# Seven-product units in single-bank PSUM tiles, hi parts one step earlier, and token-factor steps moved: a decoder layer on one core

## The chip, the cores and the metric

The kernel runs on one core of a Trainium2 chip. The metric is device time in microseconds (us) of one execution; lower is better. Three executions of the kernel before took 945.07, 948.32 and 948.42 us, so the median is 948.32 us. The profile shown here is of a fourth execution of the same program.

## What is computed

One layer of a hybrid decoder (`DEPTH = 1`) for 512 prompt tokens and 8 sample tokens that share weights, all in fp32. The mixer sub-layer joins sliding-window attention, a state-space branch and attention to 256 memory tokens. The channel sub-layer, where the change lies, is

```python
h  = rmsnorm(x, norm_ffn_g)
a  = h @ w_ffn_gate                     # 1024 -> 2816
up = h @ w_ffn_up                       # 1024 -> 2816
c  = conv_b + sum(conv_w[j] * a[t - 2 + j] for j in range(3))   # causal, along the tokens
x  = x + (gelu(c) * up) @ w_ffn_down    # 2816 -> 1024
y  = rmsnorm(x, norm_final_g)
```

## The kernel before, in words

Activations lie features by tokens: 128 features on the partitions and 520 columns, in two halves of 260 (256 prompt tokens and 4 sample tokens each). Each fp32 operand is cut into two fp32r parts, hi and lo, and each product of a 128x128 weight block with a 260-column half is three matmuls (`mm3`): hi by hi, hi by lo, lo by hi. For weights ScalarE (ACT) writes the hi part (tiles `whi`) and VectorE (DVE) then takes it from the raw weight for the lo part (`wlo`).

The channel sub-layer has three stretches.

**Plain blocks** (`for ob in range(6)`): gate (`fg`) and up (`fu`) blocks of 128 output features, 48 matmuls each, into a two-bank tile `mm` (pool `pmm`, 2 tiles). DVE moves the gate product to SBUF, the lane `conv` does the three-tap convolution (ACT, two DVE steps, small POOL steps, Gelu on ACT), and DVE then multiplies the up product in. Beside this a filler lane `y_lane` builds the token factors: four calls of `build`, each some ten DVE steps and four ACT copies, which make the four slots of sums and differences of token blocks that the next stretch multiplies by. `pump` lets a filler piece go when the planner's clocks (class `Clock`: costs by engine, plus `LAT` between engines) say that there is room; `MARG_FF` and `EV_FF` set how much, once `clk.late` is set.

**Seven-product units** (class `Strassen`, 16 of them, `fg3`, `fu3` to `fg10`, `fu10`, each for a pair of output blocks): the two output blocks by two token halves by two halves of the features are made with seven block products in place of eight. Each of the seven steps is 12 matmuls (4 factor slots by 3) into one of three accumulators:

```python
ORDER = (("A11", 0, 0, True), ("s1", 3, 2, True), ("s2", 4, 0, False), ("s4", 2, 2, False), ("s3", 5, 0, False),
         ("A12", 1, 1, True), ("A22", 6, 0, False))      # weight, token factor, accumulator, first
...
t = out_tile()
self.acc = [t[:, 0, :NH], t[:, 1, :NH], SD()[:, :NH]]
```

So accumulators 0 and 1 are the two banks of one `mm` tile and accumulator 2 is a bank of the pool `psd` (tiles `SD`, 4 of one bank). After every step `evict` adds the accumulator to where it belongs (table `EVICT`: ACT copies it out where it is the first to arrive, DVE adds or subtracts it where something is there already): A11, s1 and s2 by ACT, s4, s3 and A12 by DVE, A22 by ACT. Accumulator 0 goes on accumulating after it has been read.

**Down steps** (class `Down`), the product with `w_ffn_down` in four groups `d0` to `d3`, stand between the units by the table `FF_ORDER`. The last four blocks of `d3` run half by half at the end, beside the final norm (`finish`).

All steps of the last two stretches form one list. `s_step(s)` emits, in this order: the eviction of step s-1, the split of step s+3 (`s_split(s + D)`: ACT's hi part, DVE's lo part, then the DMA loads that this frees), and the matmuls of step s with filler pieces between them (`spump`). An engine's queue is in order, so what stands in front of a waiting instruction decides who waits. Weights come by DMAs on SP's queue, one part (`S`) also by accumulating DMAs of POOL.

Of the kernel before, what the change touches and what calls it, by code (L numbers as in the profile page):

```python
# [7 lines left out]
F32 = mybir.dt.float32  # L8
# [3 lines left out]
OP = mybir.AluOpType  # L12
# [101 lines left out]
class Clock:  # L114
# [75 lines left out]
    def op(self, eng, name, a, k):  # L190
        outs = [a[0]] + ([k["accum_out"]] if "accum_out" in k else [])
        ins = [x for x in list(a[1:]) + list(k.values()) if hasattr(x, "ap") and x is not outs[-1]]
        shape = a[0].shape
        n = 1
        for d in shape[1:]:
            n *= d
        if eng == "sp":
            out, src = a
            n = 4
            for d in out.shape:  # L200
                n *= d
            t0 = max(self.t["sp"], self.deps(eng, [out], [src]))
            self.t["sp"] = t0 + 0.45
            self.t["hw"] = max(self.t["hw"], t0 + SP_A) + max(0.26, n / 360e3)
            self.note(eng, [out], [src], self.t["hw"] + SP_B)
            return
        if eng == "pe":
            if name == "transpose":
                c = 0.9e-3 * a[1].shape[0] + 0.003
            else:  # L210
                m, w = 1, 1
                for d in a[1].shape[1:]:
                    m *= d
                for d in a[2].shape[1:]:
                    w *= d
                c = (max(0.112, 0.4434e-3 * w + 0.0045) if self.late else 0.417e-3 * max(m, w) + 0.003) \
                    if a[1].dtype == F32R else 1.667e-3 * w * (1 if m > 64 else 0.5)
        elif eng == "act":
            c = 0.833e-3 * n + 0.094 * (1 + sum(hasattr(k.get(x), "ap") for x in ("bias", "scale", "accum_out")))
            if a[1].space == PSUM:  # L220
                c -= 0.043
        elif eng == "dve":
            if name == "tensor_reduce":
                n = 1
                for d in a[1].shape[1:]:
                    n *= d
            c = 0.07 + (6.3e-3 if name == "reciprocal" else 0.52e-3 if name == "tensor_copy" and a[1].space != PSUM
                        else 1.04e-3) * n
            if name == "tensor_tensor_reduce" or name == "scalar_tensor_tensor" and hasattr(a[2], "ap"):
                c += 0.06  # L230
        elif eng == "dma":
            c = 3.3
        else:
            c = {"tensor_tensor": 0.151 + 1.95e-3 * n, "tensor_scalar": 0.215, "memset": 0.035 + 0.833e-3 * n}.get(name, 0.12 + 3.3e-3 * n)
        q = "pool" if eng == "dma" else eng
        t0 = max(self.t[q], self.deps(eng, outs, ins))
        if eng == "pe" and t0 < COLD:
            c *= 2
        end = t0 + c
        self.t[q] = t0 + 1.1 if eng == "dma" else end  # L240
        self.note(eng, outs, ins, end)
        if eng != "dma":
            self.last = max(self.last, end + self.LAT)
        else:
            self.last_dma = end
# [25 lines left out]
EV = 1.5  # L271
HZ = 2.0
EVH = 1.2
MARG_FF = -0.2
EV_FF = 1.5
MARG = -0.4
MARG_Q = -0.2
SP_A, SP_B, COLD = 1.2, 1.0, 10.0
# [11 lines left out]
def body(ctx, tc, I, O):  # L290
# [1296 lines left out]

    clk.late = True  # L1590
    pool.dma_start(O["sk"][:, :127 * 128], I["ckn"][:, 128:])
    pool.dma_start(O["sv"][:, :127 * 128], I["cvn"][:, 128:])
    B_done(2)
# [141 lines left out]
    class Strassen:  # L1735
# [18 lines left out]
                sp.dma_start(t[:, o:o + 512], s_dram(self.n, COL["A21"], 512))  # L1754
            later.append((s, lambda: pool.dma_start(t[:, 0:1024], s_dram(self.n, 512, 1024), accum_op=OP.add)))

        def split(self, p, s):
            name = ORDER[p][0]
            w = self.A(name)
            if name == "s2":  # L1760
                dve.tensor_tensor(w, w, self.A("A11"), op=OP.add)
                if self.nxt:
                    self.nxt.load("A11", s)
            elif name == "s4":
                dve.tensor_tensor(w, w, self.A("A12"), op=OP.add)
            parts_of(s, w, 512)
            if self.nxt:
                if name == "s3":
                    self.nxt.load("S", s + S_LAG)
                elif name in ("A12", "A22"):  # L1770
                    self.nxt.load(name, s)
# [18 lines left out]
        def before(self, p):  # L1790
            if p == 0:
                (fg_begin if self.kind == "fg" else fu_begin)(self.o)
                t = out_tile()
                self.acc = [t[:, 0, :NH], t[:, 1, :NH], SD()[:, :NH]]

        def go(self, p, s):
            _, f, bank, first = ORDER[p]
            for k in range(4):
                w = slice(k * P, (k + 1) * P)
                xh, xl = ysl[k].get(f)  # L1800
                mm3(self.acc[bank], HIW[s][:, w], LOW[s][:, w], xh, xl, first and k == 0, k == 3, not first)
                spump(0.36 * (3 - k))

    dcount = [0]

    class Down:
# [11 lines left out]
        def load(self, p):  # L1818
            sp.dma_start(cu[self.at[p] % 4][:, 0:self.q * P], s_dram(self.n, p * self.q * P, self.q * P))

        def split(self, p, s):
            self.steps[p] = s
            parts_of(s, cu[self.at[p] % 4][:, 0:self.q * P], self.q * P)
            j = self.at[p] + 4
            if j < len(dparts):
                dparts[j][0].load(dparts[j][1])

        def before(self, p):
            if p == 0:
                t = out_tile() if self.halves == (0, 1) or self.m % 2 == 0 else self.t0  # L1830
                if self.halves == (0,):

                    downs[self.m - 7 if self.m < 7 else -1].t0 = t
                    self.ps = [t[:, self.m % 2, :NH], None]
                    return
                self.ps = [t[:, h, :NH] for h in range(H)]
                self.both = t[:, :, :NH]

# [58 lines left out]
    steps = [(u, p) for u in units for p in range(u.n_steps)]  # L1897
    HIW, LOW = {}, {}

    def parts_of(s, src, q):  # L1900
        h, l = half("hi", s % 6)[:, 0:q], half("lo", s % 6)[:, 0:q]
        act.activation(h, src, AF.Copy)
        dve.tensor_tensor(l, src, h.bitcast(F32), op=OP.subtract)
        HIW[s], LOW[s] = h, l

    def s_split(s):
        if s < len(steps):
            u, p = steps[s]
            u.split(p, s)

    D, S_LAG = 3, 3

    def spump(rem):

# [11 lines left out]
    def s_step(s):  # L1926
        u, p = steps[s]
        if s:
            v, q = steps[s - 1]
            v.evict(q)  # L1930
        u.before(p)
        while later and later[0][0] <= s:
            later.pop(0)[1]()
        s_split(s + D)
        u.go(p, s)


# [37 lines left out]
    for ob in range(6):  # L1975
# [36 lines left out]
        if ob:  # L2012
            i = begin("fu")
            if ob == 5:
                for s in range(D):
                    s_split(s)
            pu = product(i, range(8), blk(yh, yl))
        drain([l])
        dve.tensor_tensor(hv(c), pu, hv(c), op=OP.mult)
# [72 lines left out]

    todo = finish(0, NH, (NH,))
    next(todo)
    t = None
    for i, m in enumerate((4, 5, 6, 7)):
        d = downs[m - 8]
        if i % 2 == 0:
            t = out_tile()
        d.ps[1] = t[:, i % 2, :NH]  # L2100
        d.go(0, d.steps[0], (1,))
        if m < 7:
            next(todo, None)
            x_add(m, 1)
# [145 lines left out]
```

## Time and profile before

| | us |
|---|---|
| runs of the kernel before (median) | 945.07, 948.32, 948.42 (948.32) |
| the profiled execution | 955.03 |
| its span, first to last instruction | 953.0 |
| TensorE (PE) busy / DVE / ACT / POOL | 886.5 / 603.2 / 406.6 / 151.9 |
| mean granted TensorE clock | 0.975 of full |

Every instruction of the program has line 257, that of the helper that records it, so the rows are told apart by tiles: `T` stands for the SBUF temporaries, `B` for the large buffers, `M`, `wraw`, `sv` for raw weights. A row of the chain or the timeline begins with its start and its length in us. A timeline row ends with the idle time of the engine before it and who ended it. In a wait row stand the total, the count and the longest. In a row of stages stand the stretch, its length, the busy us (and instructions) of PE, weight loads, DVE, ACT and POOL, the granted clock as a share of 2.4 GHz, the DMA share and GB/s. A matmul's end is modelled: it is drawn 0.28 us long, while the next one starts 0.12 us after it.

### The profile page before, as it was taken

How to read it: one execution, taken by the hardware profiler on the slowest of the kernel's cores; microseconds unless marked ns; L12 is line 12 of the kernel's file. 1: busy time of each engine (PE TensorE's matmuls, PEld its weight loads, DVE VectorE, ACT ScalarE, POOL GpSimd, SP SyncE). 2: the span in 40 equal slices, each digit the busy share in tenths (PEclk: the TensorE clock that was granted, in tenths of full speed). 3: DMA queues.
4: the chain of work that ended last, by engine and by line, in shares of the span. 5: the costliest groups of instructions: out<-in, count | busy, mean ns of one | idle time of the engine just before them, and what ended most of it. 6: DMA issues, size and time to landing. Idle time of an engine off the chain costs nothing.

```text
span 953.0 us, 18057 instructions
## 1 busy us (share of the span) xinstructions
PE 886.5 (93%) x7229; PEld 845.7 (89%) x7229; DVE 603.2 (63%) x1099; ACT 406.6 (43%) x797; POOL 151.9 (16%) x392
## 2 busy tenths in 40 slices
PE   9999999998999999999999999798898999899983
PEld 8998989997898998899999999788887988888973
DVE  6887678873276882126656667766676566666545
ACT  6376645453433221323333334345444445445252
POOL 7885300001000003000000101111112011111001
PEclk9999999999899998899999999899999999999987
DMA  7432572247045327052232145544546545540302
GB/s 262 163 100 90 148 166 90 90 137 141 17 136 157 107 89 174 24 185 83 90 110 89 62 125 141 137 113 131 141 109 149 135 119 132 144 112 17 120 12 90
DMA packets 52213, 110.45 MB, mean 116 GB/s; under 512 B 14001, under 2 KB 23649, under 8 KB 51857
## 3 DMA queue, kind: packets, MB, share of 16 engines
q1 hardware_dynamic: 46656, 93.73, 32.6%
q0 software_dynamic: 4240, 14.41, 8.2%
q8 instruction: 57, 0.93, 0.4%
q10 hardware_dynamic: 1232, 1.16, 0.4%
q14 instruction: 28, 0.22, 0.1%
HBM read 104.05 MB, written 6.26 MB: 116 GB/s over the span
## 4 chain that ended last, share of the span: by engine, by line
PE 66%; DVE 15%; ACT 9%; DMA 5%; issue 4%; POOL 1%; SPq 0%; DVEq 0%; ACTq 0%; POOLq 0%
PE mm L257 53%; PE SD L257 13%; DVE T L257 7%; ACT whi L257 5%; DVE wlo L257 4%; DMA wraw<-in_w 4%; ACT T L257 3%; DVE B L257 3%; DVE wraw L257 1%; DMA B<-kd 1%; ACT B L257 1%; POOL B L257 0%; SPq L257 0%; DVE TN L257 0%; DMA kd<-B 0%
## 5 line engine op out<-in xcount | busy, mean ns | idle before, releaser
L257 PE MATMUL mm<-B,whi 128*128 128x260 f32 (+1 forms) x3808 | 712.8, 289 | 48.9 <-DVE T L257 29.4
L257 PEld LDWEIGHTS mm<-B,whi 128*128 128x128 f32 x3808 | 595.4, 191 | 68.1 <-DVE T L257 19.1
L257 PE MATMUL mm<-B,wlo 128*128 128x260 f32 (+1 forms) x1904 | 542.9, 285 | 1.0 <-DVE wlo L257 1.0
L257 PEld LDWEIGHTS mm<-B,wlo 128*128 128x128 f32 x1904 | 364.1, 191 | 1.8 <-DVE wlo L257 1.7
L257 DVE TENSOR_TENSOR wlo<-wraw,whi 128x1024 fp32r<-128x1024 f32 (+1 forms) x149 | 153.5, 1031 | 150.9 <-ACT whi L257 146.4
L257 ACT ACTIVATE whi<-wraw 128x1024 fp32r<-128x1024 f32 (+1 forms) x149 | 133.4, 897 | 98.1 <-DMA wraw<-in_w 39.1
L257 ACT ACTIVATE T<-mm 128x260 f32<-128x260 f32 (+3 forms) x76 | 32.2, 446 | 87.9 <-PE mm L257 87.9
L257 DVE TENSOR_TENSOR wlo<-M,whi 128x512 fp32r<-128x512 f32 x64 | 44.3, 691 | 33.3 <-ACT whi L257 30.8
L257 ACT ACTIVATE B<-T 128x520 fp32r<-128x520 f32 (+2 forms) x48 | 29.7, 620 | 66.2 <-DVE T L257 66.2
L257 PE MATMUL SD<-B,whi 128*128 128x260 f32 x288 | 54.5, 286 | 0.2 <-DVE B L257 0.2
L257 ACT ACTIVATE whi<-M 128x512 fp32r<-128x512 f32 x64 | 39.7, 626 | 23.2 <-DVE M L257 23.2
L257 PE MATMUL SD<-B 128*64 128x72 f32 (+9 forms) x576 | 45.4, 253 | 1.9 <-DMA B<-kd 1.9
L257 PEld LDWEIGHTS SD<-B,whi 128*128 128x128 f32 x288 | 45.3, 192 | 0.4 <-DVE B L257 0.4
L257 DVE TENSOR_TENSOR B<-B 128x256 f32<-128x256 f32 (+11 forms) x78 | 36.4, 474 | 13.4 <-ACT B L257 12.0
L257 ACT ACTIVATE B<-SD 128x256 fp32r<-128x256 f32 (+6 forms) x50 | 19.0, 406 | 59.4 <-PE SD L257 59.3
L257 PEld LDWEIGHTS SD<-B 128*64 128x64 f32 (+5 forms) x576 | 31.6, 130 | 12.6 <-issue 6.1
L257 PE MATMUL SD<-B,wlo 128*128 128x260 f32 x144 | 41.1, 285 | 0.0
L257 DVE SCALAR_TENSOR_TENSOR T<-T,sm,T 128x512 f32<-128x512 f32 x44 | 33.6, 763 | 2.8 <-ACT T L257 2.6
L257 DVE TENSOR_TENSOR B<-mm,B 128x520 f32<-128x520 f32 (+3 forms) x41 | 24.6, 602 | 15.0 <-PE mm L257 15.0
L257 DVE TENSOR_TENSOR T<-T,T 128x520 f32<-128x520 f32 (+2 forms) x50 | 30.3, 606 | 5.1 <-ACT T L257 5.1
L257 POOL MEMSET T<- 128x2 f32 (+2 forms) x27 | 7.7, 285 | 159.8 <-DVE B L257 89.3
L257 DVE TENSOR_TENSOR B<-T,B 128x520 fp32r<-128x520 f32 (+2 forms) x50 | 31.4, 638 | 0.4
(166 smaller groups left out, 828.6 us busy)
## 6 DMA issues: line engine op xcount, KB each, us to landing
wraw<-in_w SPq DMA_DIRECT2D x96, 512.0 KB, 3.6
M<-in_w SPq DMA_DIRECT2D x48, 256.0 KB, 3.8
wraw<-in_w SPq DMA_DIRECT2D x36, 256.0 KB, 3.4
T<-in_w SPq DMA_DIRECT2D x36, 192.0 KB, 3.3
M<-in_w POOLq DMA_DIRECT2D x8, 512.0 KB, 6.1
wraw<-in_w POOLq DMA_DIRECT2D x8, 512.0 KB, 6.4
sv<-in_w SPq DMA_DIRECT2D x12, 192.0 KB, 3.4
B<-in_xT SPq DMA_DIRECT2D x1, 2080.0 KB, 9.4
```

Of the source, the lines that this page charges most:

```text
L257: return g(*a, **k)
```

## The change

It does three things. Accumulator 1 of a unit leaves the second bank of the `mm` tile and becomes an `SD` tile; in the same way the four half-by-half blocks at the end no longer share a tile two by two. `s_split` is cut in three (`sum`, `hi`, `lo`): the sums and the hi part of step s+4 are emitted where before all of step s+3 was; the lo part stays at s+3. And the planner's constants for the channel sub-layer change (`LAT`, ACT and DVE costs, `MARG_FF`, `EV_FF`), which sets filler pieces at other places.

```diff
-            if a[1].space == PSUM:
+            if self.late:
+                c += 0.06
+            elif a[1].space == PSUM:
                 c -= 0.043
...
-            c = 0.07 + (6.3e-3 if name == "reciprocal" else 0.52e-3 if name == "tensor_copy" and a[1].space != PSUM
+            c = (0.15 if self.late else 0.07) + (6.3e-3 if name == "reciprocal" else 0.52e-3 if name == "tensor_copy" and a[1].space != PSUM
...
-MARG_FF = -0.2
-EV_FF = 1.5
+MARG_FF = 1.0
+EV_FF = 4
...
-    clk.late = True
+    clk.late, clk.LAT = True, 0.2
...
-        def split(self, p, s):
+        def sum(self, p, s):
             name = ORDER[p][0]
-            w = self.A(name)
-            if name == "s2":
-                dve.tensor_tensor(w, w, self.A("A11"), op=OP.add)
-                if self.nxt:
+            if name in ("s2", "s4"):
+                w = self.A(name)
+                dve.tensor_tensor(w, w, self.A("A11" if name == "s2" else "A12"), op=OP.add)
+                if self.nxt and name == "s2":
                     self.nxt.load("A11", s)
-            elif name == "s4":
-                dve.tensor_tensor(w, w, self.A("A12"), op=OP.add)
-            parts_of(s, w, 512)
+
+        def hi(self, p, s):
+            hi_of(s, self.A(ORDER[p][0]), 512)
+
+        def lo(self, p, s):
+            name = ORDER[p][0]
+            lo_of(s, self.A(name), 512)
             if self.nxt:
                 if name == "s3":
                     self.nxt.load("S", s + S_LAG)
...
-                t = out_tile()
-                self.acc = [t[:, 0, :NH], t[:, 1, :NH], SD()[:, :NH]]
+                self.acc = [out_tile()[:, 0, :NH], SD()[:, :NH], SD()[:, :NH]]
...
+    def one(m):
+
+        return SD()[:, :NH] if m % 2 else out_tile()[:, 0, :NH]
...
-                t = out_tile() if self.halves == (0, 1) or self.m % 2 == 0 else self.t0
                 if self.halves == (0,):
-
-                    downs[self.m - 7 if self.m < 7 else -1].t0 = t
-                    self.ps = [t[:, self.m % 2, :NH], None]
+                    self.ps = [one(self.m), None]
                     return
+                t = out_tile()
...
-    def parts_of(s, src, q):
-        h, l = half("hi", s % 6)[:, 0:q], half("lo", s % 6)[:, 0:q]
-        act.activation(h, src, AF.Copy)
-        dve.tensor_tensor(l, src, h.bitcast(F32), op=OP.subtract)
-        HIW[s], LOW[s] = h, l
...
+    def hi_of(s, src, q):
+        HIW[s] = half("hi", s % 6)[:, 0:q]
+        act.activation(HIW[s], src, AF.Copy)
+
+    def lo_of(s, src, q):
+        LOW[s] = half("lo", s % 6)[:, 0:q]
+        dve.tensor_tensor(LOW[s], src, HIW[s].bitcast(F32), op=OP.subtract)
...
-    D, S_LAG = 3, 3
+    D, D_SUM, D_HI, S_LAG = 3, 4, 4, 3
...
-        s_split(s + D)
+        cut(s + D, "lo")
+        cut(s + D_SUM, "sum")
+        cut(s + D_HI, "hi")
         u.go(p, s)
...
-        d.ps[1] = t[:, i % 2, :NH]
+        d.ps[1] = one(m)
```

What that moves is told by three places in the order of instructions. The numbers in the names are of tiles; the line is 259 in the new text, which is two lines longer there. The words in brackets are the engines that the instruction waits for.

The first place is PE in the unit `fg4`, from the last matmul of step s3 over the step A12 to the first of A22. Before:

```order
L257 MATMUL mm_7252<-B_5921,wlo_6711 128x260
L257 MATMUL mm_7252<-B_5918,whi_6710 128x260 [waits DVE_49]
L257 MATMUL mm_7252<-B_5918,whi_6710 128x260
L257 MATMUL mm_7252<-B_5918,wlo_6711 128x260
L257 MATMUL mm_7252<-B_5919,whi_6710 128x260 x2
L257 MATMUL mm_7252<-B_5919,wlo_6711 128x260
L257 MATMUL mm_7252<-B_5920,whi_6710 128x260 x2
L257 MATMUL mm_7252<-B_5920,wlo_6711 128x260
L257 MATMUL mm_7252<-B_5921,whi_6710 128x260 x2
L257 MATMUL mm_7252<-B_5921,wlo_6711 128x260
L257 MATMUL mm_7252<-B_5918,whi_6819 128x260 [waits DVE_49,Activation_49]
```

And with the change:

```order
L259 MATMUL mm_7252<-B_5921,wlo_6723 128x260
L259 MATMUL SD_7253<-B_5918,whi_6721 128x260 x2
L259 MATMUL SD_7253<-B_5918,wlo_6723 128x260 [waits DVE_49]
L259 MATMUL SD_7253<-B_5919,whi_6721 128x260 x2
L259 MATMUL SD_7253<-B_5919,wlo_6723 128x260
L259 MATMUL SD_7253<-B_5920,whi_6721 128x260 x2
L259 MATMUL SD_7253<-B_5920,wlo_6723 128x260
L259 MATMUL SD_7253<-B_5921,whi_6721 128x260 x2
L259 MATMUL SD_7253<-B_5921,wlo_6723 128x260
L259 MATMUL mm_7252<-B_5918,whi_6811 128x260 [waits DVE_49]
```

The matmuls are the same in number and order. A12 now writes a tile of its own and its first matmul waits for nothing; its third waits for its own lo part.

The second place is ACT ahead of the first unit (`fg3`), where the last token factors (`B_5921` from `T2` tiles) are copied. Before, up to the eviction of A11:

```order
L257 ACTIVATE whi_6702<-M_5923 128x512 [waits DVE_49,PE_49]
L257 ACTIVATE B_5921<-T2_6851 128x260
L257 ACTIVATE B_5921<-T2_6852 128x520 [waits DVE_49]
L257 ACTIVATE B_5921<-T2_6853 128x520 [waits DVE_49]
L257 ACTIVATE B_5921<-T2_6898 128x520 [waits DVE_49]
L257 ACTIVATE whi_6702<-M_5923 128x512 [waits DVE_49,PE_49]
L257 ACTIVATE T2_6905<-mm_6907 128x260 [waits PE_49,Pool_49]
```

And with the change (`T2_6711` belongs to the last plain block):

```order
L259 ACTIVATE B_5921<-T2_6776 128x260 [waits DVE_49]
L259 ACTIVATE B_5921<-T2_6777 128x520 [waits DVE_49]
L259 ACTIVATE T2_6711<-T2_6711 128x520 [waits Pool_49]
L259 ACTIVATE B_5921<-T2_6778 128x520 [waits DVE_49]
L259 ACTIVATE B_5920<-T2_6711 128x520 [waits DVE_49]
L259 ACTIVATE whi_6811<-M_5924 128x512 [waits PE_49]
L259 ACTIVATE whi_6811<-M_5923 128x512 [waits DMASW3_49]
L259 ACTIVATE whi_6713<-M_5923 128x512 [waits DVE_49,PE_49] x2
L259 ACTIVATE B_5921<-T2_6900 128x520 [waits DVE_49]
L259 ACTIVATE whi_6721<-M_5923 128x512 [waits DMAHW2_49,PE_49]
L259 ACTIVATE T2_6907<-mm_6909 128x260 [waits PE_49]
```

Three of the four copies of the last factor slot now stand within the last plain block, and both hi parts that wait for a DVE sum (`whi_6713`) stand a step further ahead of the eviction.

The third place is DVE in plain block 3 (counted from 0), from the first of the two convolution steps to the multiplication with the up product (`mm`). Before:

```order
L257 SCALAR_TENSOR_TENSOR T2_6424<-T2_6423,sm_88,T2_6424 128x2x256 [waits Pool_49]
L257 TENSOR_TENSOR B_5919<-T2_6353,B_5919 128x260
L257 TENSOR_TENSOR B_5919<-T2_6354,B_5919 128x520
L257 SCALAR_TENSOR_TENSOR T2_6424<-T2_6423,sm_88,T2_6424 128x2x256 [waits DVE_49]
L257 TENSOR_TENSOR T2_6495<-T2_6354,T2_6353 128x260
L257 SCALAR_TENSOR_TENSOR T2_6495<-T2_6355,T2_6354 128x260
L257 TENSOR_TENSOR T2_6424<-T2_6424,rstd_330 128x520 [waits DVE_49,Activation_49]
L257 TENSOR_TENSOR T2_6424<-mm_6426,T2_6424 128x520 [waits DVE_49,PE_49]
```

And with the change:

```order
L259 SCALAR_TENSOR_TENSOR T2_6434<-T2_6433,sm_88,T2_6434 128x2x256 [waits Activation_49]
L259 SCALAR_TENSOR_TENSOR T2_6434<-T2_6433,sm_88,T2_6434 128x2x256 [waits DVE_49]
L259 TENSOR_TENSOR B_5919<-T2_6420,B_5919 128x520
L259 SCALAR_TENSOR_TENSOR T2_6453<-B_4921,sm_88,rstd_330 128x520
L259 SCALAR_TENSOR_TENSOR T2_6454<-B_4921,sm_88,rstd_330 128x520
L259 TENSOR_TENSOR wlo_6467<-wraw_6389,whi_6466 128x1024 [waits DMAHW6_49,Activation_49]
L259 TENSOR_TENSOR T2_6434<-T2_6434,rstd_330 128x520 [waits DVE_49,Activation_49]
L259 TENSOR_TENSOR T2_6434<-mm_6436,T2_6434 128x520 [waits DVE_49,PE_49]
```

No factor step stands between the two convolution steps any more; more of them stand behind the second one, where ACT's Gelu runs.

## Rows read from the trace of the kernel before

**Rows 1.** Page, busy time of TensorE and its weight loads.

```profile
PE 886.5 (93%) x7229; PEld 845.7 (89%) x7229; DVE 603.2 (63%) x1099; ACT 406.6 (43%) x797; POOL 151.9 (16%) x392
```

**Rows 2.** Stages: plain blocks, the 16 units, last down steps, the end.

```profile
525.00:608.80 83.80, 76.01 (x619) 74.29 (x618) 60.64 (x97) 33.90 (x54) 9.68 (x31) 0.99 0.39 111
608.80:884.40 275.60, 247.76 (x1956) 239.18 (x1956) 179.79 (x304) 125.55 (x255) 38.04 (x95) 0.99 0.47 121
884.40:916.20 31.80, 31.76 (x264) 31.66 (x264) 15.98 (x27) 11.83 (x21) 0.00 (x0) 1.00 0.27 84
916.20:953.00 36.80, 17.67 (x97) 16.25 (x96) 17.34 (x39) 11.83 (x26) 4.08 (x4) 0.72 0.18 59
```

**Rows 3.** Waits of PE in the stretch of the units, 608.8 to 884.4.

```profile
PE mm L257 <- DVE T L257: 24.9, 31, 1.5
PE mm L257 <- ACT T L257: 4.8, 9, 2.5
```

**Rows 4.** Timeline of PE in one unit, starts of A12 and A22.

```profile
650.69 0.52 PE L257 MATMUL mm<-B,whi 128*128 128x260 f32 x2 [1.54 <-DVE T L257]
...
653.02 0.48 PE L257 MATMUL mm<-B,whi 128*128 128x260 f32 x2 [0.61 <-DVE T L257]
...
653.45 0.40 PE L257 MATMUL mm<-B,whi 128*128 128x260 f32 x2
```

**Rows 5.** Timeline of DVE in the same unit.

```profile
649.74 0.56 DVE L257 TENSOR_TENSOR wlo<-sv,whi 128x384 fp32r<-128x384 f32 x1 [0.84 <-ACT whi L257]
650.22 0.42 DVE L257 TENSOR_TENSOR T<-T,mm 128x260 f32<-128x260 f32 x1
...
652.44 0.43 DVE L257 TENSOR_TENSOR T<-mm,T 128x260 f32<-128x260 f32 x1 [1.34 <-PE mm L257]
```

**Rows 6.** Waits of DVE in the stretch of the units.

```profile
DVE wlo L257 <- ACT whi L257: 70.1, 65, 2.2
```

**Rows 7.** Stages: two half-clock stretches, and one of unbroken matmuls.

```profile
607.90:614.80 6.90, 6.00 (x28) 6.00 (x29) 3.10 (x5) 4.50 (x10) 0.97 (x2) 0.51 0.42 124
400.00:500.00 100.00, 100.00 (x838) 100.00 (x837) 54.21 (x65) 35.66 (x51) 0.10 (x1) 1.00 0.34 111
918.50:925.40 6.90, 5.34 (x24) 5.27 (x24) 2.32 (x5) 2.22 (x5) 0.00 (x0) 0.51 0.00 0
```

**Rows 8.** Waits of PE in the plain blocks, 525 to 608.8.

```profile
PE mm L257 <- DVE T L257: 3.8, 4, 1.7
PE mm L257 <- ACT T L257: 2.5, 1, 2.5
```

**Rows 9.** Timeline of DVE and ACT ahead of the first unit.

```profile
605.05 1.49 DVE L257 TENSOR_TENSOR B<-T,B 128x520 fp32r<-128x520 f32 x2
...
607.84 0.63 ACT L257 ACTIVATE whi<-M 128x512 fp32r<-128x512 f32 x1 [2.04 <-DVE M L257]
608.38 0.37 ACT L257 ACTIVATE T<-mm 128x260 f32<-128x260 f32 x1
```

**Rows 10.** Timeline of PE ahead of the first unit, factor waits.

```profile
603.90 0.39 PE L257 MATMUL mm<-B,whi 128*128 128x260 f32 x1 [0.44 <-DVE B L257]
...
605.80 0.39 PE L257 MATMUL SD<-B,whi 128*128 128x260 f32 x1 [0.21 <-DVE B L257]
```

**Rows 11.** Chain in plain block 3, two factor steps between convolution steps.

```profile
569.53 0.95 DVE B L257 x2
```

**Rows 12.** Waits of PE from the last unit to the end.

```profile
PE mm L257 <- DVE B L257: 8.5, 3, 4.1
```

**Rows 13.** Chain at the end.

```profile
920.06 5.50 PE mm L257 x24
...
934.67 2.85 DVE B L257 x5
...
937.55 2.97 PE mm L257 x12
```

**Rows 14.** DMA issues: KB each, median us from issue to landing.

```profile
M<-in_w SPq DMA_DIRECT2D x48, 256.0 KB, 3.8
```

More of the change, by code (lines that the diff above doesn't have):

```diff
@@ L1819, in load, with sum, hi, lo @@
             sp.dma_start(cu[self.at[p] % 4][:, 0:self.q * P], s_dram(self.n, p * self.q * P, self.q * P))
-        def split(self, p, s):
+        def sum(self, p, s):
+            pass
+        def hi(self, p, s):
             self.steps[p] = s
-            parts_of(s, cu[self.at[p] % 4][:, 0:self.q * P], self.q * P)
+            hi_of(s, cu[self.at[p] % 4][:, 0:self.q * P], self.q * P)
+        def lo(self, p, s):
+            lo_of(s, cu[self.at[p] % 4][:, 0:self.q * P], self.q * P)
             j = self.at[p] + 4
@@ L1898, in body, with cut @@
     HIW, LOW = {}, {}
-    def parts_of(s, src, q):
-        h, l = half("hi", s % 6)[:, 0:q], half("lo", s % 6)[:, 0:q]
-        act.activation(h, src, AF.Copy)
-        dve.tensor_tensor(l, src, h.bitcast(F32), op=OP.subtract)
-        HIW[s], LOW[s] = h, l
-    def s_split(s):
+    def hi_of(s, src, q):
[5 more added lines that the diff above has]
+    D, D_SUM, D_HI, S_LAG = 3, 4, 4, 3
+    def cut(s, what):
         if s < len(steps):
             u, p = steps[s]
-            u.split(p, s)
-    D, S_LAG = 3, 3
+            getattr(u, what)(p, s)
     def spump(rem):
@@ L2014, in body @@
             if ob == 5:
-                for s in range(D):
-                    s_split(s)
+                for s in range(D_HI):
+                    cut(s, "hi")
+                    if s < D:
+                        cut(s, "lo")
             pu = product(i, range(8), blk(yh, yl))
@@ L2094, in body @@
     next(todo)
-    t = None
-    for i, m in enumerate((4, 5, 6, 7)):
+    for m in (4, 5, 6, 7):
         d = downs[m - 8]
-        if i % 2 == 0:
-            t = out_tile()
-        d.ps[1] = t[:, i % 2, :NH]
+        d.ps[1] = one(m)
         d.go(0, d.steps[0], (1,))
```

## The prediction

> **What bounds the kernel now.** I first read the page's busy times: TensorE (PE) is busy 93% of the span [rows 1], so only its idle time and its slow clock can be won. The table of stages tells where these lie [rows 2]. In the last down steps 264 matmuls take 31.76 us without a break, which is 0.120 us each, or 1.44 us for a step of 12. The 1956 matmuls of the stretch of the 16 units would take 1956 x 0.120 = 234.7 us at that pace, and take 275.6: 40.9 us are lost there. The reader should check that the waits explain this sum. In that stretch PE waits 31 times for DVE, 24.9 us, and 9 times for ACT, 4.8 us, of which 2.5 stand in front of the stretch [rows 3]. That is 27.2 us idle in 39 waits. The clock stood at half for the first 28 matmuls, which took 6.0 us [rows 7] instead of 28 x 0.120 = 3.4: 2.6 us. There remain 11.1 us, or 0.28 a wait. This is the cost that the idle column hides: a matmul is drawn 0.28 us long while the next starts after 0.12 (0.16 lost unseen), and after a wait the first two take 0.52 or 0.48 us in place of 0.40 [rows 4]. So I price every wait of PE at its idle time plus 0.28.
>
> What PE waits for is the next question. Two waits come in each unit, at the starts of A12 and A22 [rows 4]. At 650.69 A12 starts 0.05 us after DVE has finished T<-T,mm, the eviction of s3 [rows 5], although A12 writes the other bank. That eviction stood on DVE behind a lo part, and the lo part had waited 0.84 us for its hi part, which ACT had not made yet [rows 5]. At 653.02 A22 starts 0.15 us after the eviction of A12 has ended, though A22 writes the first bank. In the whole stretch DVE stands 70.1 us at lo parts whose hi part is not there [rows 6], with evictions behind them.
>
> **The change, part by part.** No matmul, copy or DMA is added or taken away; the terms are waits.
>
> *A12 and A22.* With a tile of its own A12's first matmul waits for nothing, so the whole wait goes. A22 then needs the eviction of s3 only, and has A12's 1.44 us in between. From that go 0.16 (the drawn end), 0.42 for the eviction [rows 5], and 0.05 to 0.15 to PE's start, as in the two cases above; some 0.7 us is left, in which DVE may still finish one piece of 0.55 to 0.69 us. Two such pieces in front would bring a wait back, but the hi parts are now made a step sooner, so that DVE no longer stands still in front of a lo part. I take all 31 waits as gone.
>
> The Trainium skill, page "Perfetto Trace Analysis", section "Identifying Performance Opportunities", reads a gap that repeats as a sign that there are too few buffers for the next tile, and its section "Matmul Optimizations" wants all eight PSUM banks in use. By that the change would be a loss, for it leaves a bank of each `mm` tile empty in the units; the sum would be rival 2's. The rows speak for the other reading: the tile that A12 writes was held since the unit's start, and what ended the wait was a DVE read of its other half.
>
> *The eight waits for ACT* within the units (4.8 - 2.5 = 2.3 us idle) are of s2 for the eviction of A11, which has the same slack and stood behind hi parts that waited for a sum on DVE. The sums now stand a step sooner too: I take them as gone. DVE gets denser: 179.8 us of work in some 235 us, 77% busy in place of 65%, and no engine becomes the bound. I leave 1.5 us for some five short waits of a kind I cannot see. So the units give 40.9 - 1.5 = **39.4**, the half clock's 2.6 among it. That one goes if the stall before it gets short: the granted clock was 0.51, the lower level of 1.2 GHz, behind the wait of 2.5 us here and among the waits of the end [rows 7, 8, 12], and it was 0.99 in the mean over the plain blocks with waits up to 1.7 and over the units with waits up to 1.5 [rows 2, 3, 8].
>
> *The stall ahead of the first unit*, 2.5 us [rows 8], price 2.8. The eviction of A11 stood behind a hi part, this waited for a sum, and the sum stood on DVE behind the last factor steps [rows 9]. In the new order most of these stand in the last plain block, but one hi part is still in front. I take **2.0**; bounds 0 and 2.8.
>
> *Factors that come late for the down steps:* two waits [rows 10], 0.44 + 0.21 + 2 x 0.28 = **1.2**. The two waits in front of them, for the hidden block of the last plain block, have the same chain as before and stay. Bounds -0.5 and 2.0.
>
> *The plain blocks:* four waits, 3.8 us [rows 8], price 4.9, each at a `fu` product that needs the tile of the one before. DVE empties it after the convolution. In block 3 two factor steps of 0.95 us together stood between the two convolution steps [rows 11] and now do not; in blocks 0 to 2 it is likewise, but more pieces stand behind. I take half, **2.5**; bounds 0 and 4.9.
>
> *The end:* three waits for DVE, 8.5 us [rows 12], price 8.5 + 0.84 = 9.3. In the old order two half blocks share a tile, and the second one's matmuls wait until DVE has added the first. The two other waits, 8.5 - 4.1 = 4.4 us together, go with that. The longest, 4.1, was DVE working through the first half's norm and output rows, 2.85 us in one piece of the chain [rows 13]; that work remains, and stands in front of the last sum for the norm, so the wait only moves there. I take 4.4 + 2 x 0.28 = **5.0**; bounds 0 and 9.3. Two runs of matmuls at half clock followed such waits: 24 in 5.50 us and 12 in 2.97 [rows 13], against 2.88 and 1.44, so 2.6 + 1.5 = **4.1**. No matmul of a product stands behind the wait that remains; bounds 0 and 4.1.
>
> The sum is 39.4 + 2.0 + 1.2 + 2.5 + 5.0 + 4.1 = 54.2 us. Against the profiled execution, 955.0, this gives 900.8. That execution is 6.7 us above the median of the runs, 948.3, and I set the forecast against the median: **894 us**.
>
> **The rivals.**
>
> 1. *DVE is the next in line.* At 77% it may have two pieces ahead of the eviction of s3, and A22 waits as now: 16 times 0.61 idle plus 0.28 [rows 4] is 14.2 us not won, 908. For it: DVE's queue is in order, and lo parts of the next step and conv steps lie between. Against: 70.1 us of standing still go [rows 6]. Chance 0.14.
> 2. *Too few banks.* A unit holds two of four `SD` tiles; if its s1 had to wait for the one of the unit before, each unit would get a wait the size of A12's now: 24.9 - 16 x 0.61 = 15.1 us, plus 16 x 0.28: 19.6 not won, 914. Against: four tiles hold two units, and the third matmul of A12 is the only one of that step that waits in the new order. Chance 0.04.
> 3. *It does not do what it says.* A12 would still wait, now at its third matmul for a lo part that is not ready; nothing moves but small pieces, 948. Against: the lo part was never what ended these waits [rows 3]. Chance 0.03.
> 4. *Slower: the hi part stops ACT's queue at a load.* A hi part is asked for one step sooner, while its load still starts only when an older lo part is done. In the 56 down steps the load has some three steps: from 4.3 us for the short ones. If landing took longer than that, ACT would stand, evictions behind it, and each of the 56 steps would lose up to its 1.44 us: 80.6 lost, 54.2 won, about 974. The loads of the class products land in 3.8 us [rows 14], so it decides only if they get slower as the units get closer; DMA stands at 0.47 of its share in this stretch [rows 2]. Chance 0.04.
>
> A lower clock through denser work is not among them: in 400 to 500 PE was busy without a break and the granted clock was 1.00 [rows 7].
>
> **How the numbers follow.** My forecast has 0.75, the rivals 0.14, 0.04, 0.03 and 0.04. Its own range comes from the bounds: with all of the plain blocks, the end and the first stall it is 54.2 + 2.4 + 4.3 + 0.8 + 0.8 = 62.5 won, 886; with the low bounds at the end (9.1 less) 903. To hold 8 in 10 the range must take in rival 1 and its own spread, so it is 886 to 911. About 0.5%, 4.7 us, is what a measurement of this kernel can tell from no change. Faster by more has the forecast and rivals 1 and 2: 0.93; within it rival 3: 0.03; slower rival 4: 0.04.
>
> **What would show it.** In the new profile the stretch of the 1956 matmuls should last about 236 us, with no wait above 0.5 us and the clock at 1.00. The waits of PE for DVE T should fall from 31 to a handful, those of DVE for `whi` from 70 us to less than half. In front of the first unit a wait below 1 us should remain, and none of the factor waits. At the end one wait near 4 us should stand in front of the last norm sums, on PE's row SD<-T, with no product's matmuls at half clock behind it. Waits of 0.6 us at A22 would say rival 1, waits at the first matmul of s1 rival 2, ACT waiting for sv<-in_w or T<-in_w rival 4. If the stretch takes more than 250 us, the reading of the waits is wrong.

## The result and the profile after

Four executions of the changed kernel took 894.83 to 899.09 us, median **895.85 us**, against 948.31 us of the kernel before (945.07 to 948.42). The ratio is 0.946, 95% interval 0.943 to 0.949: 52.5 us faster. The forecast was 894 us with a range of 886 to 911. The profiled execution of the changed kernel took 894.97 us with a span of 893.2; that of the kernel before was a long one (955.03), so the two traces differ by 60 us, not by 52.5.

The busy times of the page show that the work is the same (7229 matmuls, and DVE at 600.7 us where it had 603.2) and that TensorE now is busy 97% of a shorter span [rows 1]:

```profile
PE 864.1 (97%) x7229; PEld 833.1 (93%) x7229; DVE 600.7 (67%) x1099; ACT 409.5 (46%) x797; POOL 149.4 (17%) x392
```

The table of stages of the changed kernel, cut at the same matmuls as [rows 2] (plain blocks, units, last 264 matmuls, end; stretch, length, busy us of PE, weight loads, DVE, ACT, POOL, granted clock, DMA share, GB/s):

```profile
521.93:599.04 77.11, 74.86 (x618) 73.79 (x616) 59.93 (x96) 34.21 (x55) 10.14 (x31) 1.00 0.42 120
599.04:832.90 233.86, 233.81 (x1956) 233.81 (x1957) 177.83 (x303) 128.04 (x254) 35.41 (x95) 1.00 0.56 141
832.90:864.49 31.59, 31.59 (x266) 31.59 (x265) 17.34 (x29) 12.97 (x23) 0.00 (x0) 1.00 0.31 94
864.49:893.14 28.65, 13.25 (x98) 12.39 (x96) 16.25 (x37) 10.92 (x25) 4.08 (x4) 0.79 0.23 75
```

The units fell from 275.60 to 233.86 us, 41.7 less, and 1956 matmuls in 233.86 us are 0.1196 us each: nothing is left to win there but matmuls. The plain blocks fell by 6.7. From the start of the last 264 matmuls to the last instruction it was 68.6 us before (884.4 to 953.0) and is 60.2 now. The rest of the difference, 3.1 us, lies ahead of 525 us, where the change moves nothing; the section on surprises comes back to it.

The waits of PE in the four stretches of the changed kernel: none of [rows 3]'s 31 for DVE T is left. In the plain blocks the waits for DVE T [rows 8] went from 3.8 us to 1.0, and the one of 2.5 us for ACT in front of the first unit is now 0.3 us (it is counted in the second stretch).

```profile
PE mm L259 <- DVE T L259: 1.0, 2, 0.7
PE mm L259 <- ACT B L259: 0.7, 1, 0.7
PE mm L259 <- DVE B L259: 0.3, 1, 0.3
...
PE mm L259 <- ACT T L259: 0.3, 1, 0.3
...
PE SD L259 <- DVE T L259: 4.8, 2, 4.0
```

DVE still stands at lo parts in the units, but 18.1 us instead of 70.1 [rows 6]:

```profile
DVE wlo L259 <- ACT whi L259: 18.1, 27, 0.9
```

In one unit of the changed kernel (timeline of PE and DVE; idle time before a row and its cause at the row's end) A12 starts on `SD` the moment s3 is over, DVE evicts s3 as soon as PE is done with it, and A22 comes 0.81 us after that eviction has ended (647.97 - 647.16). The working of the prediction had some 0.7 there.

```profile
646.53 0.40 PE L259 MATMUL SD<-B,whi 128*128 128x260 f32 x2
...
646.73 0.43 DVE L259 TENSOR_TENSOR T<-T,mm 128x260 f32<-128x260 f32 x1 [0.48 <-PE mm L259]
...
647.97 0.40 PE L259 MATMUL mm<-B,whi 128*128 128x260 f32 x2
```

### The profile page after: what moved, and what is told of

Same layout as the page of the kernel before. It is cut to its first block, busy times and chain, and to the rows that moved or that the text cites. A ratio compares the mean times of both kernels' runs of the same rounds, so it can differ in the third digit from the quotient of the medians.

```text
span 893.2 us, 18052 instructions
## 1 busy us (share of the span) xinstructions
PE 864.1 (97%) x7229; PEld 833.1 (93%) x7229; DVE 600.7 (67%) x1099; ACT 409.5 (46%) x797; POOL 149.4 (17%) x392
## 4 chain that ended last, share of the span: by engine, by line
PE 70%; DVE 11%; issue 9%; DMA 5%; ACT 4%; POOL 1%; SPq 0%; DVEq 0%; ACTq 0%; POOLq 0%
PE mm L259 51%; PE SD L259 19%; DVE T L259 5%; DMA wraw<-in_w 3%; DVE B L259 3%; DVE wlo L259 2%; ACT T L259 2%; ACT whi L259 2%; DMA B<-kd 1%; ACT B L259 1%; POOL B L259 0%; DVE TN L259 0%; SPq L259 0%; DMA kd<-B 0%; POOL T L259 0%
## 5 line engine op out<-in xcount | busy, mean ns | idle before, releaser
L259 PE MATMUL mm<-B,whi 128*128 128x260 f32 (+1 forms) x3648 | 672.2, 285 | 7.2 <-DVE B L259 4.5
L259 PEld LDWEIGHTS mm<-B,whi 128*128 128x128 f32 x3648 | 565.5, 189 | 16.7 <-DVE B L259 5.8
L259 PE MATMUL mm<-B,wlo 128*128 128x260 f32 (+1 forms) x1824 | 516.6, 283 | 1.2 <-DVE wlo L259 1.2
L259 PEld LDWEIGHTS mm<-B,wlo 128*128 128x128 f32 x1824 | 345.6, 189 | 2.0 <-DVE wlo L259 2.0
L259 PE MATMUL SD<-B,whi 128*128 128x260 f32 x448 | 82.9, 282 | 0.0
L259 PEld LDWEIGHTS SD<-B,whi 128*128 128x128 f32 x448 | 69.1, 188 | 0.1
L259 PE MATMUL SD<-B,wlo 128*128 128x260 f32 x224 | 63.3, 282 | 0.0
L259 PEld LDWEIGHTS SD<-B,wlo 128*128 128x128 f32 x224 | 42.1, 188 | 0.0
L259 DVE TENSOR_TENSOR B<-mm,B 128x520 f32<-128x520 f32 (+2 forms) x36 | 23.0, 638 | 27.9 <-PE mm L259 27.6
```

Source lines behind the costliest of these rows:

```text
L259: return g(*a, **k)
```

## The experiments

The change has four parts that can be put in or left out one by one: banks of their own in the units, banks of their own at the end, sums and hi parts a step ahead, and the constants. Theory A is the prediction's: the shared tile makes the waits at A12 and A22, the order of sums and hi parts makes those for ACT, the constants act in the plain blocks. Each kernel ran beside the kernel before, whose median was 950.4 to 951.5 us in these sets. Stretches are cut at the same matmuls as above.

### 1. Banks of their own in the units, alone

```diff
-                t = out_tile()
-                self.acc = [t[:, 0, :NH], t[:, 1, :NH], SD()[:, :NH]]
+                self.acc = [out_tile()[:, 0, :NH], SD()[:, :NH], SD()[:, :NH]]
```

> The kernel before, with one line of the change: in the units the three accumulators lie in three banks of their own; hi parts, constants and the end are as before. Theory A (the shared tile makes the waits at A12 and A22): A12's waits go, 24.9 - 16 x 0.61 = 15.1 us idle and 15 x 0.28 = 4.2, so 19 us; of A22's 14.2 us a part goes too, since lo parts without their hi part still stand on DVE in front of evictions. 915 to 929 us. Theory B (the late lo parts make them, the tile only names them): A12 needs no eviction now but A22 still waits for the one of s3 behind a standing lo part, so the waits move from A12 to A22 and at most 5 us are won: 943 or more, with some 30 waits left.

Measured 919.4 us, ratio 0.968 (0.964 to 0.972). The units of this kernel (row of stages), and the waits of PE and of DVE in them:

```profile
606.76:850.60 243.84, 240.62 (x1956) 237.52 (x1957) 177.37 (x301) 125.11 (x254) 36.97 (x95) 0.99 0.52 135
```

```profile
PE mm L257 <- ACT T L257: 4.9, 9, 2.5
...
DVE wlo L257 <- ACT whi L257: 54.6, 65, 2.0
```

Theory A, and for A22 more than the part that it expected: all waits for evictions by DVE at A12 and at A22 went (one of 0.2 us is left in the stretch), although DVE still stood 54.6 us at lo parts. Of the 4.9 us for ACT 2.5 stand in front of the stretch, as before. Theory B falls. One line of the change gives 31.8 of the 41.7 us of the units.

### 2. Sums and hi parts a step ahead, alone

```diff
-    D, S_LAG = 3, 3
+    D, D_SUM, D_HI, S_LAG = 3, 4, 4, 3
...
-        s_split(s + D)
+        cut(s + D, "lo")
+        cut(s + D_SUM, "sum")
+        cut(s + D_HI, "hi")
```

> The change without its own banks (units and end share tiles as before) and with the old constants: only sums and hi parts stand a step sooner. Theory A: the wait at A22 stays (0.61 each, it is for A12's eviction, which starts only when A12 ends) and A12's shrinks to the same 0.6 or so, since DVE no longer stands: 24.9 - 31 x 0.61 = 6 us idle won, the ACT waits' 2.3 + 8 x 0.28 = 4.5, the first stall 2.8, half clock 2.6: about 16 us, 932 us, with some 31 waits of PE for DVE T left in the stretch. Theory B: the waits go with the standing lo parts, 39 us in the units alone: 909 us or less, with few waits left.

Measured 932.0 us, ratio 0.979 (0.976 to 0.983). Its units, and the waits of PE and DVE in them:

```profile
606.86:865.87 259.01, 242.40 (x1956) 235.68 (x1956) 180.01 (x305) 129.66 (x255) 48.36 (x95) 1.00 0.49 129
```

```profile
PE mm L257 <- DVE T L257: 16.1, 31, 0.5
...
DVE wlo L257 <- ACT whi L257: 14.5, 23, 0.8
```

The time is that of theory A, 932 us, and theory B, with 909 or less, falls. DVE hardly stands at lo parts any more (14.5 us in place of 70.1), and yet all 31 waits are there, each 0.5 us: the time from the end of one step over its eviction to the next matmul on the same tile. It is the other half of the proof: an early lo part does not take these waits away, a tile of its own does. This run also prices a wait cleanly, since its clock stood at 1.00: 259.01 - 233.86 = 25.15 us lost, 16.1 of them drawn as idle, so (25.15 - 16.1) / 31 = 0.29 us per wait that the idle column hides. The prediction had 0.28.

### 3. The constants alone

```diff
-MARG_FF = -0.2
-EV_FF = 1.5
+MARG_FF = 1.0
+EV_FF = 4
...
+            if self.late:
+                c += 0.06
...
-            c = 0.07 + (6.3e-3
+            c = (0.15 if self.late else 0.07) + (6.3e-3
...
-    clk.late = True
+    clk.late, clk.LAT = True, 0.2
```

> The kernel before with the new constants alone (the margins of the factor steps, the look at the queue, the costs of ACT and DVE operations). Theory A: they change the plain blocks only: 2.5 to 4.9 us won there, 943 to 946, the stretch of the units as before within 3 us. Rival: the constants order the small pieces in the units too, and part of the gain there is theirs: 930 or less.

Measured 952.0 us, ratio 1.000 (0.997 to 1.004). Neither theory had that: by the runs nothing is won. In the trace the plain blocks took 5.4 us less than before, the units 3.8 more, with new waits for ACT up to 4.4 us (the waits are PE's in the units):

```profile
525.78:604.20 78.42, 75.28 (x618) 74.16 (x617) 60.57 (x97) 33.69 (x54) 9.51 (x31) 1.00 0.41 118
604.20:883.56 279.36, 249.24 (x1956) 240.31 (x1956) 177.35 (x299) 124.03 (x251) 31.44 (x86) 0.98 0.46 118
```

```profile
PE mm L259 <- ACT T L259: 7.3, 3, 4.4
PE mm L259 <- ACT B L259: 2.7, 4, 1.0
```

### 4. The change without the step ahead

The changed kernel with the three depths at 3, and the calls in the order sum, hi, lo.

```diff
-    D, D_SUM, D_HI, S_LAG = 3, 4, 4, 3
+    D, D_SUM, D_HI, S_LAG = 3, 3, 3, 3
```

> The changed kernel with hi parts and sums again in the step of their lo part; banks, constants and end as changed. Theory A with both parts needed: the eight waits for ACT come back (4.5 us), the first stall (2.8) with its half clock (2.6), and a part of A22's 14.2, since lo parts stand again: 906 to 920. Rival (own banks are enough): within 3 us of the changed kernel, 893 to 899.

Measured 922.3 us, ratio 0.969 (0.966 to 0.972): 2 us above what was expected, and no faster than the banks alone (919.4). The row of its units, PE's waits there, and the timeline ahead of one of them:

```profile
601.76:857.16 255.40, 244.19 (x1956) 241.33 (x1957) 175.71 (x296) 123.47 (x251) 31.99 (x86) 0.97 0.50 129
```

```profile
PE mm L259 <- ACT T L259: 7.7, 6, 4.5
PE mm L259 <- ACT B L259: 4.0, 3, 1.8
```

```profile
675.99 0.70 DVE L259 TENSOR_TENSOR B<-T,B 128x520 fp32r<-128x520 f32 x1 [0.70 <-ACT B L259]
676.61 0.68 DVE L259 TENSOR_TENSOR wraw<-wraw,M 128x512 f32<-128x512 f32 x1
677.32 0.63 ACT L259 ACTIVATE whi<-wraw 128x512 fp32r<-128x512 f32 x1 [1.37 <-DVE wraw L259]
677.86 0.37 ACT L259 ACTIVATE T<-mm 128x260 f32<-128x260 f32 x1
...
678.28 0.59 PE L259 MATMUL mm<-B,whi 128*128 128x260 f32 x1 [4.50 <-ACT T L259]
```

Read it from the bottom. PE waited 4.5 us for the eviction of A11 (`T<-mm`). That stood on ACT behind a hi part; the hi part waited for its sum (`wraw<-wraw,M`); the sum stood on DVE behind a filler piece (`B<-T,B`), which itself waited for ACT. This is the chain of [rows 9], and with the new constants filler pieces stand in it in the units too. With the sum a step ahead the chain has 1.44 us more, and in the units of the changed kernel PE waits for it once, for 0.3 us. So the constants' gain needs the step ahead. Without it they cost in the units 3.8 of the 5.4 us that they bring in the plain blocks (experiment 3), or more than they bring: 255.4 us here against 243.8 in experiment 1, from which this kernel differs by the constants and the tiles at the end. A part of that is the clock: behind the wait of 4.5 us the granted clock was 0.50, the lower level of 1.2 GHz, for 6.0 us.

```profile
678.20:684.20 6.00, 5.92 (x27) 5.92 (x28) 2.87 (x5) 2.66 (x7) 0.60 (x2) 0.50 0.56 140
```

### 5. The change without banks of their own in the units

The line of experiment 1 put back.

> The changed kernel, but in the units A11's and A12's accumulators share a tile again. Theory A (the shared tile makes the waits): the stretch of the units is that of the run with the hi parts ahead alone, 259.0 us with 31 waits of 0.5 for DVE T, against 233.9 in the changed kernel: 895.9 + 25 = 921. Rival (with hi parts ahead and the new constants the eviction of s3 is early enough): the waits at A12 go and those at A22 stay, 15 waits at 0.5 + 0.28, 908.

Measured 923.1 us, ratio 0.970 (0.966 to 0.973). Its units and PE's waits there:

```profile
598.44:858.94 260.50, 242.39 (x1956) 235.69 (x1956) 179.33 (x305) 127.21 (x254) 36.72 (x95) 1.00 0.49 128
```

```profile
PE mm L259 <- DVE T L259: 17.6, 31, 1.2
```

The 31 waits are back, as in experiment 2, at the same hidden price: (260.50 - 233.86 - 17.6) / 31 = 0.29 us. The units alone cost 26.6 us, of the 27.3 by which the median rose.

### 6. The change with the old constants

> The changed kernel with the old constants. Theory A (constants move work of the plain blocks only): the plain blocks take 82.4 us as with the hi parts ahead alone instead of 77.1, the units 234 to 235: 901 to 902. Rival (the constants are neutral, as they were when put into the kernel before): 895 to 897, the plain blocks' 5 us coming back as waits of the units.

Measured 905.1 us, ratio 0.949 (0.945 to 0.953). Its plain blocks:

```profile
527.71:610.21 82.50, 76.12 (x618) 74.19 (x617) 59.98 (x96) 34.52 (x55) 10.22 (x31) 1.00 0.39 113
```

They take 5.4 us more than in the changed kernel; the units (233.84 us) and all behind are the same to 0.2 us. That is theory A for the stretches; its total of 901 to 902 us was missed. The median rose by 9.3 us, more than the trace can place: this execution was also 5.8 us later at the start of the plain blocks (527.71 against 521.93), where the constants are not yet in force.

### 7. The change with the old tiles at the end

```diff
-        d.ps[1] = one(m)
+        if i % 2 == 0:
+            t = out_tile()
+        d.ps[1] = t[:, i % 2, :NH]
```

(and the same for the first halves of these blocks)

> The changed kernel with the half blocks of the end in shared tiles as before. Theory A (shared tile holds back products, and the clock falls behind these waits): from the start of the last 264 matmuls to the end 65.8 to 68.5 us as in the kernel before and with the hi parts ahead alone, against 60.3: 901.5 to 904. Rival (the waits only move to the last norm sum): within 2 us of the changed kernel, 894 to 898.

Measured 903.1 us, ratio 0.948 (0.944 to 0.951). Last 264 matmuls and end, and PE's waits there:

```profile
836.84:870.45 33.61, 31.80 (x266) 31.59 (x264) 18.98 (x32) 14.03 (x25) 0.00 (x0) 1.00 0.30 89
870.45:900.71 30.26, 14.57 (x96) 13.38 (x96) 14.98 (x34) 9.90 (x23) 4.08 (x4) 0.81 0.21 71
```

```profile
PE mm L259 <- DVE B L259: 6.6, 3, 4.1
```

63.87 us against 60.24: the tiles at the end are worth 3.6 us in the traces, less than theory A's 5.5 to 8.2. The median, 903.1, does lie in theory A's range, but only half of its rise of 7.2 us is in this stretch: the plain blocks of this execution began 3.9 us later (525.83 against 521.93), where the edit moves nothing. Both expectations missed by a part: the shared tile does hold products back, but the three waits sum to 6.6 us where they were 8.5 [rows 12]. The 1.9 us between are the step ahead's: experiment 2, also with shared tiles, has the same 6.6.

### 8. Another order at the end

A try at a version faster than both kernels: the output rows of the first half (2.85 us of DVE in the chain) go behind the last half block's evictions.

```diff
-        if m < 7:
+        if m < 6:
             next(todo, None)
+        if m < 7:
             x_add(m, 1)
+    last = finish(NH, NH, (130, 130))
+    next(last)
+    next(last)
     for _ in todo:
         pass
-    for _ in finish(NH, NH, (130, 130)):
+    for _ in last:
         pass
```

> The changed kernel with another order at the end: the output rows of the first half are multiplied behind the last half block's evictions and squares, not in front of them. Theory A (the wait of 4.0 us in front of the last norm sums is DVE's 2.66 us of output rows): the wait falls to 1.3 to 1.7 us, and of the 2.4 to 2.7 us some 0.9 are given back where DVE reaches the last rows later: 1.5 us shorter, 894.4. Rival (the output's transfers set the end, since the first half's start later): no change or up to 1 us longer.

Measured 895.4 us, ratio to the kernel before 0.940 (0.937 to 0.943), beside 0.946 of the changed kernel in its own set. The two medians, 895.4 and 895.9, can't be told apart, but the traces can. The chain of the changed kernel and the row of the last eight norm matmuls behind it, and then PE's waits and the same row in this kernel:

```profile
876.96 2.85 DVE B L259 x5
```

```profile
880.70:882.60 1.90, 1.78 (x8) 1.45 (x8) 0.46 (x4) 1.02 (x5) 0.00 (x0) 0.67 0.83 278
```

```profile
PE SD L259 <- DVE T L259: 2.3, 2, 1.5
```

```profile
880.15:882.00 1.85, 1.26 (x8) 1.04 (x8) 1.85 (x5) 0.59 (x3) 0.00 (x0) 1.00 0.00 0
```

The wait fell from 4.0 to 1.5 us as theory A said, and the end became 27.40 us instead of 28.65. Not all of that is the order's. The eight matmuls behind the wait took 1.26 us in place of 1.78, but they did so in experiment 11 too, behind the unshortened wait:

```profile
883.65 1.26 PE L259 MATMUL SD<-T,ones 128*128 128x130 f32 x8 [3.96 <-DVE T L259]
```

There the end took 28.35 us, so the new order is worth an estimated 0.95 us, less than theory A's 1.5 and too small for the medians. In the other traces with the same end and the step ahead it took 28.3 to 29.0 us.

### 9 and 10. More work on DVE in front of the eviction of s3

```diff
+            if p == 4:
+                for _ in range(2):
+                    nc.vector.tensor_tensor(idle, idle, idle, op=OP.add)
```

`idle` is 128 columns that nothing else reads; experiment 10 has 4 in place of 2. One took 291 ns.

> The changed kernel with two more DVE operations per unit (128x128 on a corner of SBUF that nothing reads, some 0.25 to 0.29 us each by the 128x130 rows), in the queue just in front of the eviction of s3. Theory A (A22 has 0.7 to 0.8 us left after that eviction, and DVE idles some 0.5 in front of it): no wait comes back, the units take 234 to 236 us, 895 to 898 in all. Rival 1 of the prediction (DVE is the next in line): each of the 16 units gets a wait of 0.1 to 0.5 at A22, 16 x (0.3 + 0.28) = 9 us, 905.

> The same with four such operations, 1.0 to 1.16 us. Theory A: where DVE had no idle time in front of the eviction A22 waits 0.3 to 0.4, some half of the units: 8 x (0.4 + 0.28) = 5 us, units 237 to 242 us, 899 to 904. Rival (DVE's share of busy time is what counts, 82% instead of 76%): no wait, 896.

Measured 896.4 us, ratio 0.943 (0.937 to 0.948), and 902.1 us, ratio 0.948 (0.944 to 0.953). The units with two more operations and with four, and then PE's waits for DVE in the same order:

```profile
596.61:831.20 234.59, 234.28 (x1956) 233.94 (x1957) 184.43 (x334) 127.92 (x254) 35.78 (x95) 1.00 0.54 140
```

```profile
603.38:843.60 240.22, 236.33 (x1956) 234.31 (x1956) 193.16 (x366) 128.12 (x254) 35.34 (x95) 1.00 0.53 138
```

```profile
PE mm L259 <- DVE T L259: 0.3, 1, 0.3
```

```profile
PE mm L259 <- DVE T L259: 3.5, 8, 0.9
```

Two cost 0.7 us in all 16 units together and bring one wait of 0.3 us. Four bring a wait at A22 in half the units and 6.4 us, near what theory A gave for them. So in half the units the margin in front of A22 lies between about 0.6 and 1.2 us, and in the other half above that: rival 1 did not come, but was little more than 0.6 us a unit away. It is the place in the queue that decides and not the busy share, which would have let both pass (193.16 / 240.22 is 80%).

### 11. A12 in the second `mm` tile

```diff
-                self.acc = [out_tile()[:, 0, :NH], SD()[:, :NH], SD()[:, :NH]]
+                self.acc = [out_tile()[:, 0, :NH], out_tile()[:, 0, :NH], SD()[:, :NH]]
```

> The changed kernel, but A12's accumulator is the first half of the second mm tile, the other half of which stays empty, instead of a bank of SD: each unit now holds both mm tiles and two banks of them are empty. Theory A (only the tile of its own counts): units 233.9 us, 895.9. Rival 2 of the prediction (too few banks): the next product after a unit waits for an mm tile, at 16 ends of units 0.6 + 0.28, 14 us, 910.

Measured 896.2 us, ratio 0.942 (0.937 to 0.947). The units:

```profile
601.92:835.78 233.86, 233.81 (x1956) 233.81 (x1957) 177.77 (x303) 128.04 (x254) 35.76 (x95) 1.00 0.54 141
```

They are the same to 0.01 us, with two half-empty `mm` tiles in each unit. Rival 2 falls: the one wait of PE in the units of the changed kernel is at an `mm` tile and not at the `SD` tile of s1, and here two empty banks bring none. The Trainium skill's wish for all eight banks (page "Perfetto Trace Analysis", section "Matmul Optimizations") is not borne out by this pair of runs: banks left empty cost nothing measurable. The Trainium skill's other sentence, that independent groups should rotate through different banks (section "Matmuls" of the same page), was kept by the kernel before too, as A11 and A12 had two banks; what held them together was that the two banks were one tile. The wait stood in the program, as a wait for DVE at A12's first matmul, and it went with a tile of its own, be that of `SD` or the second `mm` tile.

### 12. The change with the old costs, new margins

The lines of experiment 3 put back, but for `MARG_FF` and `EV_FF`.

> The changed kernel with the new margins but the old costs of ACT and DVE operations and the old latency. Theory A (the margins bring the factor steps forward): plain blocks 77 to 78 us, total 896 to 898. Rival (the costs do it: they tell the planner that DVE is late): plain blocks 82, 901 to 906, as with all constants old.

Measured 906.3 us, ratio 0.952 (0.947 to 0.957). Its plain blocks and PE's waits there:

```profile
528.11:611.43 83.32, 76.90 (x618) 75.61 (x618) 60.96 (x97) 34.50 (x55) 9.62 (x31) 0.98 0.40 111
```

```profile
PE mm L257 <- ACT B L257: 3.1, 1, 3.1
PE mm L257 <- DVE T L257: 2.9, 3, 1.3
```

Theory A on the margins falls: without the higher costs and the new latency the new margins bring nothing to the plain blocks, 83.3 us. The rival has it, but for 0.3 us in the total. Whether the costs alone would do was not tried.

## Why the prediction was right, and where it was not

The forecast of 894 us is 2 us from the median, and the sum of 54.2 us stands against 52.5 by the medians. That it is so near is in part luck. Read off the two traces the three groups of terms below give 41.7 + 6.7 + 8.4 = 56.8 us, 2.6 more than forecast. The terms came from an execution 6.7 us above the median, and the sum was then set against the median; but of the 59.8 us between the two spans only 3.1 lie outside the terms. Term by term, by the two profiled executions and the runs:

- *Units, 39.4 forecast, 41.7 measured.* Right in size. The pace taken from the last down steps (0.120 us) held to 0.0004 us, and the hidden 0.28 us a wait measured 0.29 twice (experiments 2 and 5). The reserve of 1.5 us for waits of a kind that couldn't be seen was not needed. Together with the slightly faster pace that is the difference. **The step that failed** is the reason given for A22: that the hi parts a step sooner were needed so that DVE reaches the eviction of s3 in time. Experiment 1 shows A22 free without them, with DVE standing 54.6 us. What they give in the units is the rest, 243.84 - 233.86 = 10.0 us (the constants give nothing there, experiment 6): the waits for ACT, and the half clock behind the first stall. Experiment 2 shows 16.6 us for them alone, since they also shorten the waits at A12 to 0.5 us where the tile is shared; the two parts overlap by 31.8 + 16.6 - 41.7 = 6.7 us.
- *First stall 2.0, factor waits 1.2, plain blocks 2.5: 5.7 forecast, 6.7 measured.* The stall of 2.5 us became one of 0.3, a little better than the value taken, and the factor waits went. The plain blocks were mis-sized: half of the four waits was taken, and their idle time went from 3.8 us to 1.0. Experiments 6 and 12 place most of this stretch's gain with the constants, 5.4 us. The prediction treated these as a matter of the plain blocks alone; experiments 3 and 4 show that in the units they do harm where sums are not ahead. It did not forecast this, because it priced only the whole change.
- *The end, 5.0 and 4.1 for the clock: 9.1 forecast, 8.4 measured.* PE's idle time there fell from 8.5 to 4.8 us with one wait fewer, which is 3.7 + 0.28 = 4.0 us; the 4.4 us that remain are, as an estimate, the clock's. One wait of 4.0 us is left in front of the last norm sums, as forecast, and it is the first half's output rows (experiment 8). But the 4.4 us of idle time of the two other waits were put down to the tiles as a whole: 1.9 of them go with the step ahead (experiment 7), and a new wait of 0.8 us, at the first norm sum, was not forecast.
- *The rivals.* DVE next in line had a margin of some 0.6 us a unit (9, 10). Too few banks did not show (11). Rival 4 would have put loads in front of ACT: in the units of the changed kernel no wait of ACT for a load is in the list, and the loads of the class products land in 3.7 us (3.8 before [rows 14]).

What stays open: which of the costs and margins the plain blocks need, and how much of 9.3 us in experiment 6 beyond the 5.4 in its trace is scatter.

## What to carry to other kernels

A wait is put down to the instruction that ended it; ask also whether the two sides touch the same bytes or only the same tile. Here one line that gave an accumulator a tile of its own was worth 31 us, with no work removed. Where one engine's queue hangs on a sum of another engine, put the sum a step ahead first and add filler work beside it afterwards: the same constants were worth nothing without that order and 5.4 us with it.

## What was not expected

- The stretches that the change touches repeat closely: the plain blocks took 77.1 to 77.2 us in each of the profiled executions with the new constants and the step ahead, and the units 233.84 to 233.86 us in five of the six kernels with own banks, the step ahead and no added work (236.17 in experiment 12, with three more waits for ACT). The scatter of the total comes from ahead of them: the plain blocks start at 519.52 us in one profiled execution (experiment 9) and at 528.11 in another (experiment 12), with the same 4297 matmuls in front:

```profile
0.00:519.52 519.52, 508.56 (x4297) 479.99 (x4298) 328.85 (x638) 223.28 (x442) 100.80 (x262) 0.99 0.41 121
```

```profile
0.00:528.11 528.11, 514.30 (x4297) 484.23 (x4298) 329.16 (x637) 223.34 (x442) 100.56 (x262) 0.98 0.41 119
```

  A part of this is the granted clock (0.99 and 0.98); what sets it was not tried.
- A wait of one length is not always followed by the half clock. In experiments 2 and 7 the last half blocks begin after the same wait for the same eviction, 1.86 us long, and the 5.2 us from there were at 0.67 of full clock in the mean in the one and at 1.00 in the other:

```profile
899.60:904.80 5.20, 4.65 (x24) 4.47 (x24) 1.71 (x4) 1.81 (x5) 0.00 (x0) 0.67 0.00 0
```

```profile
870.45:875.65 5.20, 4.54 (x36) 4.39 (x37) 2.15 (x5) 3.31 (x7) 0.00 (x0) 1.00 0.00 0
```

  The eight last norm matmuls show the same: behind the same wait of 4.0 us they took 1.26 us in experiments 5 and 11, and 1.68 to 2.10 us in five other traces.
